# A third column group with seven products in the second eighth of an MLP, and its sums of activations in two parts

## The chip, the cores and the metric

The kernel runs on one core of one Trainium2 chip. The metric is the device time of one execution in microseconds. Before the change it is 2023.43 us, the median of three runs (2023.22 to 2023.98).

## The reference, cut to what matters

A trunk of two layers on 256 tokens of width 2048, all in float32. The change lies in the MLP that ends each layer:

```python
h2 = rms_norm(x, norm2_g[l])
x = x + jnp.square(jax.nn.relu(h2 @ w_up[l])) @ w_down[l]      # w_up 2048 x 8192, w_down 8192 x 2048
```

## The kernel before, in words

**Precision.** Every operand of a product stands as a high part (rounded to fp32r) and a low part (what is left). A product is three multiplications on TensorE: high by high, high by low, low by high. For weights, ScalarE makes the high part (`high`, L168, for a half tile L186) and VectorE the low part (`low`, L178 and L191). Weight tiles are 128 x 1024 numbers, loaded by SP into `raw` (7 buffers); `hi` and `lo` have 6 buffers each.

**The MLP in eighths.** The 8192 hidden columns are worked in eight parts of 1024. Eighth e first does w_up for its own 1024 columns: four blocks of 256 columns, each block in four steps, 16 steps in all, numbered from 0 in this text. A block's two halves add up in one PSUM bank (`acc0` or `acc1`, by turns); `after_up` then has ScalarE take it out with a Relu (L787), square it (L790) and make its high part (L646), and VectorE its low part (L649). Then come the steps of w_down for the eighth before, whose hidden columns are ready. So "the second eighth" (e = 1) multiplies w_up for its own columns and w_down for the first eighth's.

**Seven products.** An ordinary step (`transposed`, L410) is one weight tile and 24 multiplications with 256 moving columns. For 512 output columns of one eighth of w_down that makes 4 steps. A column group in `fast` (L414 to 452, multiplications at L440) does the same in two steps by seven products of half-size blocks instead of eight. Such a seven-product step takes two weight tiles, `top` and `bottom`, and makes two more from them, `upper` and `lower`: four subtractions on VectorE (L219, L220, L223, L224), and a high and a low part of each. Its 42 multiplications go through the products in this order: top; bottom twice; upper twice; lower twice. It also needs sums of activations: `sums` (L800) forms four sums and differences of the hidden blocks on VectorE (L803 to L806) and splits them into high and low parts in `shared` (L646, L649). `sums_ready` (L435) has them recorded ahead of the step.

**Where these steps stand.** The three column groups are numbered 1, 2, 3 here (g = 0, 1, 2 in the code) and cover columns 0 to 511, 512 to 1023 and 1024 to 1535. `ORDER` and `USUAL` (L63 to 66) give, for each eighth and group, the two ordinary steps ahead of which its two seven-product steps are put; such a place is called a position below. `USUAL` is ((7, 9), (2, 3), (13, 14)). The second eighth has an entry of its own with two groups. Columns outside the groups go through ordinary steps behind step 15.

**What becomes of the results.** Group 1 stays in PSUM over all eighths. Groups 2 and 3 take three banks (the one of `acc0` and `acc1` that is not in use, `acc2`, `acc3`) and half a bank for the seventh product; behind their second step ScalarE copies the three banks to `stage` (L908), later the seventh (L894), and POOL sends them to DRAM, the first time plainly and then adding (L873). Group 1 and group 3 share the half bank of the seventh product, which ScalarE empties for group 1 by L876. Ordinary columns up to 1535 are scaled and added to x by VectorE (L768, L510), those from 1536 are kept in `rest_sums` (L771 for e = 1, else L774).

**What sets the order.** The program is written out by hand. At each step the main loop first records the high parts up to five tiles past the step's first one, then what has come due (`soon`), the low parts up to four tiles past it, further due calls (`behind`), loads, and the multiplications; then `after`, and as much of the queue of `later` as a budget allows:

```python
            high_to(done + 2 + ahead)
            run_due()
            low_to(done + 1 + ahead)
            run_due(behind)
            load_more()
            mm()
```

The engines then run their own instructions in this order. So ScalarE's L787 of a block stands behind all high parts of weights that were recorded before that block's last multiplications.

Of the kernel before, what the change touches and what calls it, by code (L numbers as in the profile page):

```python
# [29 lines left out]
F32R = mybir.dt.float32r  # L30
I32 = mybir.dt.int32
AF = mybir.ActivationFunctionType
OP = mybir.AluOpType
AX = mybir.AxisListType

P = 128
# [3 lines left out]
KC = D // P  # L40
NH = 8
# [18 lines left out]

ORDER = {1: ((7, 10), (13, 14)), 6: ((12, 15), (2, 3), (7, 8)), 7: ((7, 10), (2, 3)), 8: ()}  # L63
FINAL = (7, 7, 6)
LAST = (4, 6, 8, 10, 0, 2, 12, 14)
USUAL = ((7, 9), (2, 3), (13, 14))
# [25 lines left out]
def trunk(ctx: ExitStack, tc: tile.TileContext, layout, xT, consts, gains, w, b_sp, w_sp, out):  # L92
    nc = tc.nc
# [18 lines left out]
    shared = [None]  # L112
    ar = tp.tile([P, sum(a[1] * a[2] for a in ARENA.values()) - FIRST], F32, name="ar")
    inner_flat = ar[:, 0:2048]
    inner = inner_flat.rearrange("p (k t) -> p k t", k=NH)
# [3 lines left out]
    def new_shared(dtype):  # L119

        shared[0] = tp.tile([P, FIRST], dtype, name="shared", tag="shared", bufs=1)
# [106 lines left out]
    cols = cp.tile([P, (2 * DEPTH + 1) * KC + 2 * DEPTH * NH], F32, name="cols")  # L228
# [14 lines left out]
    def later(delay, cost, fn):  # L243

        queue.append((now[0] + delay, cost, fn))
# [118 lines left out]
    summed, sum_parts = [True], [None]  # L364
# [4 lines left out]
    def collect(fn, *args, **kw):  # L369
        n = len(steps)  # L370
        fn(*args, **kw)
        part = steps[n:]
        del steps[n:]
        return part
# [100 lines left out]
    def mark(fn):  # L475

        steps.append((None, fn, None))
# [4 lines left out]
    def from_tiles(tiles, n):  # L482
        return lambda k: tiles[k // n][0][:, k % n, :, :]

    def new_half(cell):
        cell[0] = tp.tile([P, NH, 2, S], F32R, name="half", tag="half", bufs=2)
# [15 lines left out]
    def pair(ps):  # L502
        return ps.rearrange("p (a b) -> p a b", a=2)
# [14 lines left out]
    def layer(l, n1, n2, n3, last):  # L518
# [125 lines left out]
        def to_half(t, c, src, wait=False):  # L644

            act.activation(t[:, c:c + 2, 0, :], src, AF.Copy)  # L646

            def low():
                vec.tensor_tensor(t[:, c:c + 2, 1, :], src, t[:, c:c + 2, 0, :].bitcast(F32), op=OP.subtract)  # L649

            if wait:
                behind.append((now[0] + 1, low))
            else:
                low()
# [98 lines left out]
        def wide(t):  # L753
            return t[:, None, :].to_broadcast([P, 2, S])
# [8 lines left out]
        def after_down(e, c, ps):  # L763

            if e == 8:
                update(n3, c, ps, True, last)
            elif c < 12:
                vec.tensor_tensor(pair(ps), pair(ps), wide(n2.R2), op=OP.mult)  # L768
                update(n3, c, ps, False, last)
            elif e == 1:  # L770
                act.activation(rest_sums[:, c - 12:c - 10, :], pair(ps), AF.Copy)  # L771
            else:
                y = rest_sums[:, c - 12:c - 10, :]
                vec.tensor_tensor(y, y, pair(ps), op=OP.add)  # L774
# [6 lines left out]
        def after_up(e):  # L781
            def f(c, ps):
                if hid[e][0] is None:
                    new_half(hid[e])
                z = inner[:, c // P:c // P + 2, :]
                if e < 7:
                    act.activation(z, pair(ps), AF.Relu)  # L787
                else:
                    vec.scalar_tensor_tensor(z, pair(ps), 0.0, wide(n2.R), op0=OP.max, op1=OP.mult)
                act.activation(z, z, AF.Square)  # L790
                to_half(hid[e][0], c // P, z, True)
                if c == 768:
                    summed[0] = False
                    if e == 0:
                        new_shared(F32R)
                        sum_parts[0] = shared[0].rearrange("p (k h t) -> p k h t", k=NH, h=2)
                    later(1, 1.5, sums)
            return f

        def sums():  # L800

            a11, a12, a21, a22 = (inner[:, 4 * k:4 * k + 4, t * P:(t + 1) * P] for t in range(2) for k in range(2))
            vec.tensor_tensor(a22, a21, a22, op=OP.add)  # L803
            vec.tensor_tensor(a21, a11, a21, op=OP.subtract)
            vec.tensor_tensor(a11, a22, a11, op=OP.subtract)
            vec.tensor_tensor(a12, a12, a11, op=OP.subtract)  # L806

            def parts(k):
                to_half(sum_parts[0], k, inner[:, k:k + 2, :])
                summed[0] = k == 6  # L810

            for k in range(0, 8, 2):
                later(0, 0.6, lambda k=k: parts(k))

        def combine(place, c, banks, o=None):

# [46 lines left out]
        def slots_other(g, banks):  # L863
            seventh = sevenths()[g - 1]
            banks[:] = [acc_bank(1 - bank_at[0]), acc_bank(2), acc_bank(3)]
            return [h for b in banks for h in halves(b)] + [seventh]

        far = [dp.tile([P, 256 if g == 0 else 7 * 256], F32, name=f"far{l}{g}") for g in range(3)]

        def put(e, g, r):  # L870

            src = stage[:, r] if g else stage_one
            nc.gpsimd.dma_start(far[g][:, r], src, **({} if e == max(g, 1) else {"accum_op": OP.add}))  # L873

        def seventh_out(e, o):
            act.activation(stage_one, o[6], AF.Copy)  # L876
            put(e, 0, slice(0, 256))

        def first_done(e):
            def f(o):  # L880
                if e < 7:
                    soon(5, lambda: seventh_out(e, o))
                else:
                    soon(10, lambda: nc.gpsimd.dma_start(stage[:, 1536:1792], far[0]))
                    soon(15, lambda: combine(stage, 0, [aux_bank] * 2, o))
                    for i, c in enumerate((12, 14)):
                        soon(17 + 2 * i, lambda c=c: rest_in(c))
            return f

        def other_done(e, g, banks):  # L890
            here = [lambda i=i: acc_bank(i) for i in (2, 3)]

            def rest(o):
                act.activation(stage[:, 1536:1792], o[6], AF.Copy)  # L894
                for i in range(4):
                    soon(2 * i, lambda r=slice(512 * i, min(512 * (i + 1), 1792)): move(r))
                if e == FINAL[g]:
                    soon(9, lambda: combine(stage, 4 * g, here))

            def move(r):  # L900
                if e < FINAL[g]:
                    put(e, g, r)
                else:
                    nc.gpsimd.dma_start(stage[:, r], far[g][:, r], accum_op=OP.add)

            def f(o):
                for i in range(3):
                    act.activation(stage[:, 512 * i:512 * (i + 1)], banks[i], AF.Copy)  # L908
                soon(5, lambda: rest(o))
            return f  # L910

        base = len(steps)
        for e in range(9):
            up, down, quick = [], [], []
            if e == 8:
                mark(lambda: bank_at.__setitem__(0, 1))
            if e < 8:
                up = collect(transposed, "w_up", l, 0, KC, e * 1024, 1024, from_hs, after_up(e), of=2)
            if e:
                w = 512 * len(ORDER.get(e, USUAL))  # L920
                hidden = [hid[e - 1]]
                down = collect(transposed, "w_down", l, (e - 1) * 1024, 8, w, D - w, from_tiles(hidden, NH),
                               lambda c, ps, e=e, w=w: after_down(e, (c + w) // P, ps),
                               apart=last and e == 8, of=2 if e < 8 else 4,
                               cols=None if e < 8 else [c * P for c in LAST])
                for g, at in enumerate(ORDER.get(e, USUAL)):
                    banks = []
                    quick += zip(at, collect(fast, "w_down", l, (e - 1) * 1024, 512 * g, hidden,
                                             (lambda g=g, banks=banks: slots_other(g, banks)) if g else slots_first,
                                             (0, 2, 4, 6) if g or e == 1 else (6,), range(7) if g or e == 7 else (6,),  # L930
                                             other_done(e, g, banks) if g else first_done(e)))
            quick = dict(quick)
            for i, one in enumerate(up + down):
                if i in quick:
                    steps.append(quick[i])
                steps.append(one)
# [13 lines left out]
    for l in range(DEPTH):  # L950
        layer(l, norms[2 * l], norms[2 * l + 1], norms[2 * l + 2], l == DEPTH - 1)
# [80 lines left out]
    n = norms[-1]  # L1032
# [3 lines left out]
    for c, w in [(0, 1), (1, 1)] + [(c, 2) for c in range(2, KC, 2)]:  # L1036
        r = slice(c, c + w)
# [38 lines left out]
```

## Time and profile before

| | us |
|---|---|
| median of three runs | 2023.43 |
| the profiled execution | 2023.7 |
| its span, first to last instruction | 2021.9 |
| TensorE busy | 2009.5 |
| VectorE busy | 1579.8 |
| ScalarE busy | 1221.2 |

In the profile PE is TensorE (its multiplications overlap, so that one is listed longer than its distance to the next), PEld its weight loads, DVE VectorE, ACT ScalarE, POOL GpSimd. "L178" is a line of the kernel. In a row of a timeline stand the start, the length, engine, line, operation, what it writes and reads, the count, and in brackets how long the engine was idle before and what ended that.

### The profile page before, as it was taken

To read this page: it belongs to the slowest core of one execution; us is meant where nothing else is said; L and a number is where in the kernel's file an instruction comes from. 1 tells how busy PE (TensorE), PEld (TensorE's weight loads), DVE (VectorE), ACT (ScalarE), POOL (GpSimd) and SP (SyncE) were. 2 spreads that over 40 slices of the span, in tenths; PEclk is the share of its full clock that TensorE was granted. 3 is DMA by queue.
4 is the path that set the end of the run, shared out by engine and by line. 5 is a ranking of instruction groups with operands and counts; after the bars stand their busy time and mean duration, and the time that the engine had idled before them with its cause. 6 is when DMAs were issued, how large, how long until landed. Compare 5 with 4: busy or idle time off the path is not lost.

```text
span 2021.9 us, 40716 instructions
## 1 busy us (share of the span) xinstructions
PE 2009.5 (99%) x16810; PEld 1973.4 (98%) x16810; DVE 1579.8 (78%) x1954; ACT 1221.2 (60%) x1613; POOL 156.2 (8%) x200
## 2 busy tenths in 40 slices
PE   9999999999999999999999999999999999999997
PEld 8998999999999999999989989999999999999997
DVE  7566766688888898898856667667888898888985
ACT  7565455566566666665645654556666666667653
POOL 0002300000001000100000032000000000010000
PEclk9999999999999999999999999999999999999998
DMA  9555556566678776866664555565676776777662
GB/s 330 192 167 167 187 189 202 174 229 204 222 219 239 240 225 203 249 215 215 201 215 158 168 187 188 188 199 179 217 229 208 228 236 216 239 220 241 212 215 81
DMA packets 126442, 419.26 MB, mean 207 GB/s; under 512 B 14128, under 2 KB 22064, under 8 KB 126256
## 3 DMA queue, kind: packets, MB, share of 16 engines
q1 hardware_dynamic: 110800, 389.86, 57.2%
q0 software_dynamic: 14304, 23.86, 6.5%
q8 instruction: 131, 2.15, 0.4%
q10 hardware_dynamic: 1152, 2.94, 0.4%
q14 instruction: 55, 0.45, 0.1%
HBM read 394.58 MB, written 22.02 MB: 206 GB/s over the span
## 4 chain that ended last, share of the span: by engine, by line
PE 99%; DVE 0%; ACT 0%; issue 0%; DVEq 0%
PE acc L410 70%; PE acc L440 10%; PE aux L440 8%; PE acc L470 3%; PE acc L472 3%; PE acc L471 3%; PE aux L699 0%; PE aux L635 0%; PE aux L593 0%; PE aux L622 0%; PE aux L994 0%; DVE x L1038 0%; PE aux L596 0%; PE aux L637 0%; PE acc L846 0%; PE aux L539 0%
## 5 line engine op out<-in xcount | busy, mean ns | idle before, releaser
L168 ACT ACTIVATE hi<-raw 128x1024 fp32r<-128x1024 f32 (+1 forms) x817 | 836.9, 1050 | 487.5 <-DVE raw L220 216.2
L178 DVE TENSOR_TENSOR lo<-raw,hi 128x1024 fp32r<-128x1024 f32 (+1 forms) x817 | 965.3, 1214 | 143.4 <-ACT hi L168 140.4
L410 PE MATMUL acc<-hs,hi 128*128 128x256 f32 x5632 | 985.9, 277 | 0.0
L410 PEld LDWEIGHTS acc<-hs,hi 128*128 128x128 f32 x5632 | 857.9, 188 | 0.4 <-issue 0.2
L410 PE MATMUL acc<-hs,lo 128*128 128x256 f32 x2816 | 778.0, 276 | 0.0
L410 PEld LDWEIGHTS acc<-hs,lo 128*128 128x128 f32 x2816 | 528.7, 188 | 0.4 <-issue 0.2
L410 PE MATMUL acc<-half,hi 128*128 128x256 f32 x2688 | 462.2, 276 | 0.0
L410 PEld LDWEIGHTS acc<-half,hi 128*128 128x128 f32 x2688 | 406.7, 188 | 0.0
L410 PE MATMUL acc<-half,lo 128*128 128x256 f32 x1344 | 371.0, 276 | 0.0
L410 PEld LDWEIGHTS acc<-half,lo 128*128 128x128 f32 x1344 | 252.3, 188 | 0.0
L873 POOL DMA_DIRECT2D far<-ar x92 | 74.2, 816 | 1164.4 <-ACT ar L876 563.9
L440 PE MATMUL acc<-hi,shared 128*128 128x256 f32 x768 | 138.4, 276 | 0.0
L440 PEld LDWEIGHTS acc<-hi,shared 128*128 128x128 f32 x768 | 119.2, 188 | 0.0
L440 PE MATMUL aux<-hi,half 128*128 128x256 f32 x528 | 110.6, 276 | 0.0
L440 PE MATMUL acc<-lo,shared 128*128 128x256 f32 x384 | 106.0, 276 | 0.0
L649 DVE TENSOR_TENSOR half<-ar,half 128x512 fp32r<-128x512 f32 x72 | 49.8, 691 | 68.6 <-ACT half L646 68.6
L470 PE MATMUL acc<-hi,hs 128*128 128x512 f32 x256 | 101.8, 398 | 0.0
L472 PE MATMUL acc<-hi,hs 128*128 128x512 f32 x256 | 100.6, 393 | 0.0
L471 PE MATMUL acc<-lo,hs 128*128 128x512 f32 x256 | 100.3, 392 | 0.0
L440 PEld LDWEIGHTS aux<-hi,half 128*128 128x128 f32 x528 | 87.2, 188 | 0.0
L440 PE MATMUL aux<-hi,shared 128*128 128x256 f32 x448 | 80.7, 276 | 0.0
L510 DVE TENSOR_TENSOR x<-x,acc 128x512 f32<-128x512 f32 (+1 forms) x49 | 33.1, 675 | 59.1 <-PE acc L410 57.3
(150 smaller groups left out, 1955.3 us busy)
## 6 DMA issues: line engine op xcount, KB each, us to landing
raw<-in_w SPq DMA_DIRECT2D x731, 512.0 KB, 4.7
far<-ar POOLq DMA_DIRECT2D x60, 256.0 KB, 8.3
far<-ar POOLq DMA_DIRECT2D x32, 128.0 KB, 4.3
ar<-far POOLq DMA_DIRECT2D x12, 256.0 KB, 9.7
raw<-in_w SPq DMA_DIRECT2D x10, 256.0 KB, 5.1
x<-in_xT SPq DMA_DIRECT2D x7, 256.0 KB, 5.9
out<-x SPq DMA_DIRECT2D x7, 256.0 KB, 3.1
shared<-in_b_sp ACTq DMA_DIRECT2D x2, 512.0 KB, 7.7
```

The costliest lines, as they stand in the source:

```text
L168: act.activation(self.h[:, j * m:(j + 1) * m], self.raw[:, j * m:(j + 1) * m], AF.Copy)
L178: vec.tensor_tensor(lo[:, r], self.raw[:, r], self.h[:, r].bitcast(F32), op=OP.subtract)
L410: pe.matmul(o, lhsT=lhs, rhs=xs[:, rhs, :], start=(first and j == 0), stop=(last and j == 2), skip_group_check=True)
L440: calls.append(lambda k=k, j=j, lhs=lhs, rhs=rhs: pe.matmul(o[n], lhsT=lhs, rhs=rhs, start=(p == 0 and k == 0 and j == 0 and n in fresh), ...
L470: pe.matmul(ps, lhsT=xh, rhs=hi, start=(k0 + k == 0), stop=False)
L471: pe.matmul(ps, lhsT=xh, rhs=lo, start=False, stop=False)
L472: pe.matmul(ps, lhsT=xl, rhs=hi, start=False, stop=(k0 + k == KC - 1))
L510: vec.tensor_tensor(xj, xj, ps[j][:, 0:S] if alone else pair(ps)[:, j, :], op=OP.add)
L649: vec.tensor_tensor(t[:, c:c + 2, 1, :], src, t[:, c:c + 2, 0, :].bitcast(F32), op=OP.subtract)
L873: nc.gpsimd.dma_start(far[g][:, r], src, **({} if e == max(g, 1) else {"accum_op": OP.add}))
```

## The change

`ORDER` has three groups for the second eighth, at (9, 11), (5, 6) and (13, 14); before there were two, at (7, 10) and (13, 14). Its ordinary columns of w_down shrink from 1024 to 512. Group 3's first transfer to DRAM now happens in the second eighth. In the first eighth the blocks of w_up come in the order 0, 512, 256, 768; the sums of activations are formed in two parts: one behind block 512, from blocks 0 and 512, and one behind block 768, from the other two.

```diff
-ORDER = {1: ((7, 10), (13, 14)), 6: ((12, 15), (2, 3), (7, 8)), 7: ((7, 10), (2, 3)), 8: ()}
+ORDER = {1: ((9, 11), (5, 6), (13, 14)), 6: ((12, 15), (2, 3), (7, 8)), 7: ((7, 10), (2, 3)), 8: ()}
@@ after_up
                 to_half(hid[e][0], c // P, z, True)
+                if e == 0 and c == 512:
+                    new_shared(F32R)
+                    sum_parts[0] = shared[0].rearrange("p (k h t) -> p k h t", k=NH, h=2)
+                    later(1, 1.0, lambda: sums([0]))
                 if c == 768:
                     summed[0] = False
-                    if e == 0:
-                        new_shared(F32R)
-                        sum_parts[0] = shared[0].rearrange("p (k h t) -> p k h t", k=NH, h=2)
-                    later(1, 1.5, sums)
+                    later(1, 1.5, lambda: sums([0, 1] if e else [1]))
-        def sums():
-            a11, a12, a21, a22 = (inner[:, 4 * k:4 * k + 4, t * P:(t + 1) * P] for t in range(2) for k in range(2))
+        def sums(ps):
+            n, i = 2 * len(ps), 2 * ps[0]
+            a11, a12, a21, a22 = (inner[:, 4 * k + i:4 * k + i + n, t * P:(t + 1) * P] for t in range(2) for k in range(2))
@@ sums
             for k in range(0, 8, 2):
-                later(0, 0.6, lambda k=k: parts(k))
+                if k % 4 // 2 in ps:
+                    later(0, 0.6, lambda k=k: parts(k))
@@ put
-            nc.gpsimd.dma_start(far[g][:, r], src, **({} if e == max(g, 1) else {"accum_op": OP.add}))
+            nc.gpsimd.dma_start(far[g][:, r], src, **({} if e == 1 else {"accum_op": OP.add}))
@@ the loop over eighths
-                up = collect(transposed, "w_up", l, 0, KC, e * 1024, 1024, from_hs, after_up(e), of=2)
+                up = collect(transposed, "w_up", l, 0, KC, e * 1024, 1024, from_hs, after_up(e), of=2,
+                             cols=None if e else (0, 512, 256, 768))
```

VectorE at the turn from the first to the second eighth of layer 0, from the last operation of four on the sums to the last subtraction for the first seven-product step (`lo` are low parts of weights, `half` of activations, `shared` of their sums). Before:

```order
L806 TENSOR_TENSOR ar<-ar 128x4x128
L178 TENSOR_TENSOR lo<-raw,hi 128x1024
L649 TENSOR_TENSOR shared<-ar,shared 128x2x256 x2
L178 TENSOR_TENSOR lo<-raw,hi 128x1024
L649 TENSOR_TENSOR shared<-ar,shared 128x2x256 x2
L191 TENSOR_TENSOR lo<-raw,hi 128x512
L178 TENSOR_TENSOR lo<-raw,hi 128x1024
L219 TENSOR_TENSOR raw<-raw 128x2x256
```

And now, with all four operations on the second half of the sums:

```order
L805 TENSOR_TENSOR ar<-ar 128x2x128
L806 TENSOR_TENSOR ar<-ar 128x2x128
L807 TENSOR_TENSOR ar<-ar 128x2x128
L808 TENSOR_TENSOR ar<-ar 128x2x128
L191 TENSOR_TENSOR lo<-raw,hi 128x512
L649 TENSOR_TENSOR shared<-ar,shared 128x2x256 x2
L178 TENSOR_TENSOR lo<-raw,hi 128x1024
L219 TENSOR_TENSOR raw<-raw 128x2x256
```

The operations on the sums are half as wide, two of the four pairs of low parts have moved ahead, and two ordinary tiles (L178) fewer stand before the step's own.

ScalarE in the same eighth, from the `lower` tile of one seven-product step to what follows the four high parts of position 13 (the numbers tell the tiles apart; L186 is the `top` of position 13; `acc1` is the bank of columns 512 to 767 of w_up; L876, now L879, empties the seventh product of group 1). Before, behind position 10:

```order
L168 ACTIVATE hi_4565<-raw_4306 128x1024
L168 ACTIVATE hi_4597<-raw_4406 128x1024
L168 ACTIVATE hi_4627<-raw_4436 128x1024
L168 ACTIVATE hi_4673<-raw_4466 128x1024
L186 ACTIVATE hi_4675<-raw_4532 128x512
L168 ACTIVATE hi_4677<-raw_4534 128x1024
L168 ACTIVATE hi_4689<-raw_4532 128x1024
L168 ACTIVATE hi_4723<-raw_4534 128x1024
L876 ACTIVATE ar_80<-aux_4471 128x256
L787 ACTIVATE ar_80<-acc1_4572 128x512
```

And now, behind position 11:

```order
L168 ACTIVATE hi_4738<-raw_4578 128x1024
L168 ACTIVATE hi_4774<-raw_4580 128x1024
L168 ACTIVATE hi_4804<-raw_4613 128x1024
L186 ACTIVATE hi_4850<-raw_4648 128x512
L168 ACTIVATE hi_4852<-raw_4680 128x1024
L168 ACTIVATE hi_4862<-raw_4648 128x1024
L168 ACTIVATE hi_4866<-raw_4680 128x1024
L787 ACTIVATE ar_80<-acc1_4650 128x512
L790 ACTIVATE ar_80<-ar_80 128x512
L646 ACTIVATE half_4370<-ar_80 128x2x256
L168 ACTIVATE hi_4903<-raw_4744 128x1024
L879 ACTIVATE ar_80<-aux_4415 128x256
```

Two ordinary tiles instead of three now stand between the two seven-product steps, and the copy of group 1's seventh product has moved from ahead of L787 to behind it.

## The prediction

> **What bounds the kernel now.** I read the page first, then TensorE's waits, then the busy time stage by stage, then the engines' timelines around the second eighth of the MLP. The page has the span, the engines and the chain that ended last.
>
> ```profile
> span 2021.9 us, 40716 instructions
> PE 2009.5 (99%) x16810; PEld 1973.4 (98%) x16810; DVE 1579.8 (78%) x1954; ACT 1221.2 (60%) x1613; POOL 156.2 (8%) x200
> PE 99%; DVE 0%; ACT 0%; issue 0%; DVEq 0%
> ```
>
> TensorE is the chain. The view of waits, for TensorE alone, has two rows, both outside the MLP's eighths:
>
> ```profile
> PE aux L328 <- DVE nr L354: 1.2, 1, 1.2
> PE aux L994 <- DVE warm L990: 1.1, 1, 1.1
> ```
>
> So the kernel's time is the number of multiplications times their pace, and an edit can gain only by removing multiplications, and lose only by making TensorE wait. Busy time by stage (columns: stretch, length, PE, PEld, DVE, ACT, POOL, granted clock, DMA share, GB/s), for the first eighth, the second, and the third of layer 0:
>
> ```profile
> 333.20:376.80 43.60, 43.60 (x386) 43.60 (x385) 26.14 (x36) 23.62 (x31) 0.00 (x0) 1.00 0.60 193
> 376.80:461.10 84.30, 84.30 (x745) 84.30 (x744) 71.98 (x84) 54.50 (x69) 2.96 (x5) 1.00 0.59 201
> 461.10:544.20 83.10, 83.10 (x735) 83.10 (x734) 69.48 (x78) 54.41 (x69) 6.60 (x9) 1.00 0.72 227
> ```
>
> The second eighth, which has seven products in two column groups, lasts 84.3 us; the third, which has them in all three, 83.1. TensorE is busy throughout all three at full clock. VectorE has slack in the first eighth (26 of 43.6 us) and little later (72 of 84).
>
> **What is removed.** Group 3 costs 4 ordinary steps of 24 multiplications, 96, before; now 2 seven-product steps of 42, 84. That is 12 fewer in each layer, 24 in all. Their pace, from the first seven-product multiplication of the third eighth and of the fourth, in TensorE's timeline:
>
> ```profile
> 466.44 0.28 PE L440 MATMUL acc<-hi,half 128*128 128x256 f32 x1
> 549.52 0.28 PE L440 MATMUL acc<-hi,half 128*128 128x256 f32 x1
> ```
>
> One eighth with three groups is (16 + 4) x 24 + 6 x 42 = 732 multiplications, and 83.08 / 732 = 0.1135 us each. So 24 x 0.1135 = 2.72 us go, 1.36 in each layer. An ordinary step takes 2.72 us, a seven-product step 4.77.
>
> The Trainium skill (TensorE: Matmul & The Clock Gate, "Wait — 56ns, not 53.3ns?") puts the distance of warm multiplications at N / 2.4 GHz plus about 2.5 ns. By that, an estimate from that page, 256 columns take 109.2 ns and the change removes 2.62 us; the trace has 113.5 ns, so the measurement decides.
>
> **What is added beside TensorE, and where it lies.** Each seven-product step needs, from VectorE, low parts of four weight tiles and four subtractions, and from ScalarE four high parts. Group 3's two steps cost VectorE more than its four ordinary tiles did, so VectorE's work per stretch is the matter. In the third eighth (the nearest row of an eighth with three groups) its work for one such step and what follows reads:
>
> ```profile
> 490.90 1.23 DVE L178 TENSOR_TENSOR lo<-raw,hi 128x1024 fp32r<-128x1024 f32 x1 [0.20 <-ACT hi L168]
> 492.04 0.68 DVE L191 TENSOR_TENSOR lo<-raw,hi 128x512 fp32r<-128x512 f32 x1
> 492.94 1.23 DVE L178 TENSOR_TENSOR lo<-raw,hi 128x1024 fp32r<-128x1024 f32 x1 [0.21 <-ACT hi L168]
> 494.08 0.68 DVE L219 TENSOR_TENSOR raw<-raw 128x512 f32<-128x512 f32 x1
> 494.80 0.69 DVE L220 TENSOR_TENSOR raw<-raw 128x512 f32<-128x512 f32 x1
> 495.52 0.69 DVE L223 TENSOR_TENSOR raw<-raw 128x512 f32<-128x512 f32 x1
> 496.25 0.69 DVE L224 TENSOR_TENSOR raw<-raw 128x512 f32<-128x512 f32 x1
> 496.86 2.52 DVE L178 TENSOR_TENSOR lo<-raw,hi 128x1024 fp32r<-128x1024 f32 x2
> 499.97 0.69 DVE L649 TENSOR_TENSOR half<-ar,half 128x512 fp32r<-128x512 f32 x1 [0.59 <-ACT half L646]
> 500.92 4.63 DVE L178 TENSOR_TENSOR lo<-raw,hi 128x1024 fp32r<-128x1024 f32 x4 [0.26 <-ACT hi L168]
> ...
> 517.01 0.69 DVE L191 TENSOR_TENSOR lo<-raw,hi 128x512 fp32r<-128x512 f32 x1
> ...
> 521.53 4.77 DVE L178 TENSOR_TENSOR lo<-raw,hi 128x1024 fp32r<-128x1024 f32 x4
> ```
>
> From the top's low part (492.04) to the end of lower's (499.38) are 7.34 us, 0.29 of it a wait; without it 7.05, which I take (top 0.61, bottom 1.14, subtractions 2.78, upper and lower 2.52). The step at 517.01 took 6.9. An ordinary tile takes 1.14. So from position 9 to 15, with four seven-product and seven ordinary steps, VectorE has 4 x 7.05 + 7 x 1.14 + 2 x 0.69 = 37.6 us of work, and TensorE 4 x 4.77 + 7 x 2.72 = 38.1. There is next to no room for waits there; before, only three seven-product steps (10, 13, 14) lay in that stretch.
>
> **First place: the sums, position 5.** TensorE starts the second eighth at 376.8 and now reaches its first seven-product step at 376.8 + 5 x 2.72 = 390.4, where before it was position 7. ScalarE, then VectorE, at that place before, and a 256-wide VectorE operation:
>
> ```profile
> 376.80 0.60 ACT L787 ACTIVATE ar<-acc 128x512 f32<-128x512 f32 x1 [1.66 <-PE acc L410]
> 378.63 2.00 ACT L168 ACTIVATE hi<-raw 128x1024 fp32r<-128x1024 f32 x2
> 387.68 0.60 ACT L787 ACTIVATE ar<-acc 128x512 f32<-128x512 f32 x1 [1.66 <-PE acc L410]
> ...
> 378.76 0.69 DVE L649 TENSOR_TENSOR half<-ar,half 128x512 fp32r<-128x512 f32 x1 [2.36 <-ACT half L646]
> 392.08 3.49 DVE L178 TENSOR_TENSOR lo<-raw,hi 128x1024 fp32r<-128x1024 f32 x3
> ...
> L826 DVE TENSOR_TENSOR ar<-ar 128x256 f32<-128x256 f32 x6 | 2.5, 417 | 0.0
> ```
>
> Half of the sums is now done in the first eighth, in VectorE's slack, at no cost. The rest, from 379.45: four 256-wide operations (0.45 each with the gap) to 381.3, the top's low part 381.9, two low parts of sums 383.2, bottom 384.3, subtractions 387.1, upper 388.3, lower 389.6. TensorE reads upper after 18 multiplications (392.4) and lower after 30 (393.8): 4 us in hand, so no wait. Before, upper and lower came out of the row at 392.08, for a step at 395.8: as much in hand. The bank that the step takes is free when ScalarE's L787 is through, about 388.9: 1.5 us in hand.
>
> **Second place: ScalarE between positions 6 and 13.** Behind group 2, ScalarE copies three banks and cannot get on with weights until TensorE is through. That is shown in the third eighth behind position 3, which ended at 478.7:
>
> ```profile
> 478.22 0.60 ACT L908 ACTIVATE ar<-acc 128x512 f32<-128x512 f32 x1 [0.76 <-PE acc L440]
> 478.72 2.00 ACT L168 ACTIVATE hi<-raw 128x1024 fp32r<-128x1024 f32 x2
> 480.62 0.62 ACT L186 ACTIVATE hi<-raw 128x512 fp32r<-128x512 f32 x1
> 486.24 0.37 ACT L894 ACTIVATE ar<-aux 128x256 f32<-128x256 f32 x1
> ...
> 497.06 1.06 ACT L168 ACTIVATE hi<-raw 128x1024 fp32r<-128x1024 f32 x1 [0.39 <-DVE raw L224]
> 498.02 0.58 ACT L787 ACTIVATE ar<-acc 128x512 f32<-128x512 f32 x1
> 498.63 0.64 ACT L790 ACTIVATE ar<-ar 128x512 f32<-128x512 f32 x1
> 499.30 0.63 ACT L646 ACTIVATE half<-ar 128x512 fp32r<-128x512 f32 x1
> 499.84 3.89 ACT L168 ACTIVATE hi<-raw 128x1024 fp32r<-128x1024 f32 x4
> 512.96 0.60 ACT L787 ACTIVATE ar<-acc 128x512 f32<-128x512 f32 x1 [1.61 <-PE acc L410]
> ...
> 479.81 2.36 DVE L178 TENSOR_TENSOR lo<-raw,hi 128x1024 fp32r<-128x1024 f32 x2 [2.62 <-ACT hi L168]
> ```
>
> VectorE stood for 2.62 us and started again 1.1 us behind the step's end. Call that end R. There, four ordinary steps lie between this and the next seven-product step; now it is three (6, 7, 8), then 9, 11, 13 and 14. TensorE gets to position 9 at R + 8.2, to 11 at 18.4, to 13 at 28.6, to 14 at 36.1. VectorE's side:
>
> Step 8's tile ends at 2.25, position 9's four at 9.3; lower is read at 11.6: 2.3 in hand. ScalarE's lower (7.0) is followed by a copy (0.3), L787, L790, L646 (497.06 to 499.84 is 2.78 for a weight tile and these three), so step 9's weights start there at 10.1, and VectorE (1.08 later, as from 499.84 to 500.92) ends at 12.3; read at 12.9: 0.6 in hand. Step 10 ends at 13.45, position 11's upper at 19.15 (read at 20.4), lower at 20.5. Steps 11 and 12 end at 22.75, position 13's subtractions at 27.3. Now ScalarE's lower high part runs from 27.4 to 28.35, and only then L787 of columns 512 to 767, which empties the bank that group 3's first product takes: to 28.95. TensorE is there at 28.6. It waits 0.35, with the handover 0.4. In the third eighth L787 itself waited for TensorE (512.96), so nothing waited for it. Behind it step 13's tile ends at 32.45 (read at 33.8), position 14's upper at 38.2 (read at 38.5): 0.3 in hand. Then the order is that of later eighths.
>
> So each layer gains 1.36 and loses 0.4. The wait's bounds: with 6.9 us for each of the three seven-product steps ahead, VectorE is 0.45 earlier and the wait is gone; with 7.34 it is 0.87 later and the wait 1.3. I take 0.4, by the 7.05 of rows without waits.
>
> **At nothing.** Four more bank copies per layer on ScalarE are in the walk above. Four more transfers per layer are issued on POOL, busy 3 of 84 us there. SP's loads keep number and order; a weight buffer is loaded again seven loads later, over 10 us, and no TensorE wait for weights is in the rows above. The vector updates of columns 1024 to 1535 (four operations per layer) go, behind position 15, where nothing waits for them. Turning the first eighth's blocks moves the same 384 multiplications. If VectorE's slack there were gone, the half sums would cost up to their 4 x 0.45 us, but 17 us are idle.
>
> **Sum.** The profiled execution took 2023.7 (span 2021.9 and 1.8 around it), 0.3 over the median, 2023.43. 2 x (1.36 - 0.4) = 1.9: 2021.8 for such an execution, 2021.5 against the median. About 0.2% (4.0 us) is what a measurement of this kernel can tell from no change; all of the removed work is less than that.
>
> **Rivals.**
> No wait (0.25): VectorE is half a microsecond earlier, L787 is through in time, the whole 2.72 shows: 2020.7. For it: TensorE waits nowhere in any eighth now. Against it: no eighth has this spacing.
> VectorE falls behind (0.20), the one that ends slower: at positions 9, 11 and 13 it waits for ScalarE as at 499.97 and 500.92 (0.59 + 0.26 us), 2.5 us in all; all of it adds to the lateness at position 13, 0.4 + 2.5 = 2.9 us in each layer: 2023.43 - 2.72 + 5.8 = 2026.5. It decides from 1.36 us per layer (slower than before), and from 3.4 it passes 0.2%. For it: 37.6 us of work in 38.1. Against it: some of these waits are in the walk already.
> The Trainium skill (same page, "Part 1: The HAM clock gate") states that TensorE falls to half clock after an idle window of about 3.4 us. The granted clock was 1.00 in each stage above; by an estimate from that page a wait beyond that would cost another 1.7 us, which no run here shows yet.
> It does not do what it says (0.05): another wait eats just what is gained, 2023.4.
>
> **Numbers.** The forecast (a wait of 0.1 to 1.3 per layer, 2021.0 to 2023.3) has 0.50. The range runs from 2020.4 (no wait, less the runs' spread of 0.2 to 0.3) to 2024.2, into the first third of VectorE's case; it leaves out some 0.15. Faster by over 0.2% needs more than all removed work: 0.01. Slower by over 0.2%: the far quarter of VectorE's case, 0.05. Within: 0.94.
>
> **What would show it.** Right: 24 fewer multiplications; the second eighth at about 83.3 us; TensorE's waits have a row at L440 or L410 behind ScalarE's L787 near position 13, 0.4 us in each layer; none at position 5. Wrong: a wait at position 5 on the sums; waits on L178 at 9, 11 or 14 of more than 1.3 us; a third eighth longer than 83.1.

## The result, and the profile after

The changed kernel takes 2054.98 us (median of 5 runs, 2053.74 to 2055.56); the kernel before took 2023.6 beside it (2023.22 to 2023.98). The ratio is 1.0155, with an interval of 1.0141 to 1.0168: 31.4 us slower, where the prediction had 2 us faster. The profiled execution took 2054.98, its span 2053.2.

The page and TensorE's waits look like those of before. The page's span, engines and granted clock, then the one row that is new in the view of waits (PEld are weight loads; the columns are us in total, times, longest; the view of before has no row at L440, and the view of the multiplications alone, PE, has the same two rows as before, since the wait stands at a weight load):

```profile
span 2053.2 us, 40733 instructions
PE 2040.8 (99%) x16786; PEld 2004.3 (98%) x16786; DVE 1595.6 (78%) x1978; ACT 1233.7 (60%) x1629; POOL 162.8 (8%) x208
PEclk9999999999999999999999999999999999999999
```

```profile
PEld acc L440 <- ACT ar L787: 0.6, 2, 0.3
```

There are 24 multiplications fewer (16786 for 16810), one new wait of 0.3 us in each layer, at a seven-product step behind ScalarE's L787, and a granted clock at 0.9 or more throughout. Yet TensorE is busy for 31.3 us longer. Nothing in these views says where. The busy time by stage does, in the same columns as before (first eighth and third):

```profile
333.40:377.00 43.60, 43.60 (x386) 43.60 (x385) 28.89 (x42) 24.71 (x33) 0.00 (x0) 1.00 0.62 195
...
460.80:547.10 86.30, 86.30 (x735) 86.30 (x734) 72.33 (x82) 55.66 (x70) 7.82 (x9) 1.00 0.73 218
```

The first eighth takes the same 43.60 us for the same 386 multiplications. The third takes 86.30 for 735, where before it took 83.10 for 735. The clock is 1.00 in both. So each multiplication takes longer, with nothing to wait for. Grouped by operation over one stretch of 10 us (500 to 510), before and after, with the mean length in ns last ahead of the idle time:

```profile
L410 PE MATMUL acc<-hs,hi 128*128 128x256 f32 x32 | 5.7, 276 | 0.0
```

```profile
L410 PE MATMUL acc<-hs,hi 128*128 128x256 f32 x30 | 5.6, 281 | 0.0
```

The chain in order of time (start, length, what) shows from where to where. A stretch of ordinary multiplications divided by its count gives the pace. Before, in the third eighth:

```profile
478.99 10.78 PE acc L410 x95
```

After, from the start of layer 0's MLP to its end (rows are left out in between; L849, before L846, are the transposes that `turn_back` makes in the eighth eighth; "turned blocks" below):

```profile
341.61 48.98 PE acc L410 x432
480.05 11.20 PE acc L410 x95
566.34 11.20 PE acc L410 x95
849.28 11.20 PE acc L410 x95
884.53 0.44 PE acc L849 x4
890.87 8.18 PE acc L410 x72
```

48.98 / 432 is 113.4 ns. Then 11.20 / 95 is 117.9, the same from the third eighth to the eighth, and behind the turned blocks (four transposes at 884.53, four more at 890.43) it is 8.18 / 72 = 113.6 again. TensorE's timeline at position 13 of the second eighth has the place where it begins (rows that hold two multiplications are left out), and ScalarE's timeline what it waited for:

```profile
430.74 0.28 PE L410 MATMUL acc<-hs,lo 128*128 128x256 f32 x1
431.08 0.28 PE L410 MATMUL acc<-hs,lo 128*128 128x256 f32 x1
431.19 0.28 PE L410 MATMUL acc<-hs,hi 128*128 128x256 f32 x1
431.59 0.39 PE L440 MATMUL acc<-hi,half 128*128 128x256 f32 x1
431.81 0.28 PE L440 MATMUL acc<-lo,half 128*128 128x256 f32 x1
432.17 0.28 PE L440 MATMUL acc<-lo,half 128*128 128x256 f32 x1
432.52 0.28 PE L440 MATMUL acc<-lo,half 128*128 128x256 f32 x1
```

```profile
429.99 1.06 ACT L168 ACTIVATE hi<-raw 128x1024 fp32r<-128x1024 f32 x1 [0.39 <-DVE raw L224]
430.96 0.58 ACT L787 ACTIVATE ar<-acc 128x512 f32<-128x512 f32 x1
```

Every third multiplication, the one with a low part of the weights, has a row of its own here. Up to 431.08 these stand 0.34 us apart, from 431.81 on 0.35 to 0.36. Between lies the predicted wait: 431.19 + 0.11 would be 431.30, and TensorE starts at 431.59, when L787 (done at 431.54) has freed the bank.

So the 31 us are a slower pace from that wait to the turned blocks, in each layer: one eighth is 566.34 - 480.05 = 86.29 us, 3.21 over the 83.08 of before. From position 13 of the second eighth to the first turned blocks are about 3,843 multiplications, 5.25 eighths of 732, so 16.9 us in each layer and 33.7 in both. Less the 2.7 removed and with 0.6 of wait, that makes 31.6; the medians differ by 31.4.

### The profile page after: what moved, and what is told of

It reads as the page before. It is cut to its first block, busy times and chain, and to the rows that moved or that the text cites. A ratio compares the mean times of both kernels' runs of the same rounds, so it can differ in the third digit from the quotient of the medians.

```text
span 2053.2 us, 40733 instructions
## 1 busy us (share of the span) xinstructions
PE 2040.8 (99%) x16786; PEld 2004.3 (98%) x16786; DVE 1595.6 (78%) x1978; ACT 1233.7 (60%) x1629; POOL 162.8 (8%) x208
## 4 chain that ended last, share of the span: by engine, by line
PE 96%; DVE 2%; ACT 1%; issue 1%; DVEq 0%; ACTq 0%
PE acc L410 67%; PE acc L440 11%; PE aux L440 7%; PE acc L470 3%; PE acc L472 3%; PE acc L471 3%; ACT hi L168 1%; DVE lo L178 0%; PE aux L699 0%; PE aux L635 0%; PE aux L593 0%; PE aux L622 0%; PE aux L998 0%; DVE x L1042 0%; DVE raw L224 0%
## 5 line engine op out<-in xcount | busy, mean ns | idle before, releaser
L178 DVE TENSOR_TENSOR lo<-raw,hi 128x1024 fp32r<-128x1024 f32 (+1 forms) x821 | 970.3, 1214 | 153.2 <-ACT hi L168 149.7
L410 PE MATMUL acc<-hs,hi 128*128 128x256 f32 x5632 | 1003.8, 279 | 0.0
L410 PE MATMUL acc<-half,hi 128*128 128x256 f32 x2560 | 444.9, 278 | 0.0
L410 PEld LDWEIGHTS acc<-half,hi 128*128 128x128 f32 x2560 | 388.6, 188 | 0.0
L410 PE MATMUL acc<-half,lo 128*128 128x256 f32 x1280 | 355.0, 277 | 0.0
L410 PEld LDWEIGHTS acc<-half,lo 128*128 128x128 f32 x1280 | 241.7, 189 | 0.0
L876 POOL DMA_DIRECT2D far<-ar x100 | 80.7, 810 | 1187.4 <-ACT ar L911 772.1
L440 PE MATMUL acc<-hi,shared 128*128 128x256 f32 x832 | 154.5, 279 | 0.0
L440 PEld LDWEIGHTS acc<-hi,shared 128*128 128x128 f32 x832 | 130.4, 188 | 0.0
L440 PE MATMUL aux<-hi,half 128*128 128x256 f32 x544 | 116.5, 279 | 0.0
L440 PE MATMUL acc<-lo,shared 128*128 128x256 f32 x416 | 115.9, 279 | 0.0
L440 PEld LDWEIGHTS aux<-hi,half 128*128 128x128 f32 x544 | 90.4, 188 | 0.0
L440 PE MATMUL aux<-hi,shared 128*128 128x256 f32 x448 | 82.8, 278 | 0.0
L440 PE MATMUL acc<-hi,half 128*128 128x256 f32 x416 | 81.8, 280 | 0.2
```

Source lines behind the costliest of these rows:

```text
L178: vec.tensor_tensor(lo[:, r], self.raw[:, r], self.h[:, r].bitcast(F32), op=OP.subtract)
L410: pe.matmul(o, lhsT=lhs, rhs=xs[:, rhs, :], start=(first and j == 0), stop=(last and j == 2), skip_group_check=True)
L440: calls.append(lambda k=k, j=j, lhs=lhs, rhs=rhs: pe.matmul(o[n], lhsT=lhs, rhs=rhs, start=(p == 0 and k == 0 and j == 0 and n in fresh), ...
L876: nc.gpsimd.dma_start(far[g][:, r], src, **({} if e == 1 else {"accum_op": OP.add}))
```

## The experiments

The theory (the first in the expectations): TensorE runs these multiplications at either of two paces. A standstill sets the slower one, and it stays until multiplications of another kind come, as the transposes of the turned blocks are. The rival: it is the added work (a third seven-product group in the second eighth, the sums in two parts, what VectorE, ScalarE and the transfers do beside TensorE) that slows each multiplication. The expectations are quoted as they stood before each run.

**The third group later, no wait.**

```diff
-ORDER = {1: ((9, 11), (5, 6), (13, 14)), 6: ((12, 15), (2, 3), (7, 8)), 7: ((7, 10), (2, 3)), 8: ()}
+ORDER = {1: ((9, 11), (5, 6), (14, 15)), 6: ((12, 15), (2, 3), (7, 8)), 7: ((7, 10), (2, 3)), 8: ()}
```

> The changed kernel with group 3 at positions 14 and 15 of the second eighth in place of 13 and 14, nothing else. ScalarE's L787 is then through 2.3 us before TensorE wants the bank. Theory 1 (a standstill of TensorE leaves it at a slower pace, 117.8 ns for a multiplication of 256 columns in place of 113.3, until multiplications of another kind come): no wait, no slower pace, 2023.6 less 2.7: 2020.9 us. Theory 2 (the third group's work for VectorE, ScalarE and POOL in the second eighth, or the order of the groups and the sums in two parts, slow the multiplications): that work is all still there, so 2050 to 2055 us with multiplications at 117.8 ns.

Measured: 2020.48 us (2019.83 to 2021.17), ratio to before 0.9986 (0.9977 to 0.9995); span 2018.6. The weight loads' waits have no row at L440, and the chain of this run has the step itself and the third eighth at the faster pace:

```profile
434.13 4.08 PE acc L440 x36
477.83 10.78 PE acc L410 x95
```

All the added work is still there, one step later, and the time is 34.5 us shorter. The rival falls. The difference to before, 3.0 us, is the 2.72 of the removed multiplications within the runs' spread. This kernel beats both.

**The kernel before with a wait.** Five copies of a constant onto itself on ScalarE, ahead of L787 of columns 512 to 767 in the second eighth; nothing of the change.

```diff
+                if e == 1 and c == 512:
+                    for _ in range(5):
+                        act.activation(con[:, 0:512], con[:, 0:512], AF.Copy)
```

> The kernel before, with five more copies of 512 columns on ScalarE (a constant onto itself) ahead of L787 of columns 512 to 767 in the second eighth of each layer, so that TensorE has to wait some 0.4 us for the bank at position 13. TensorE's program is that of before. Theory 1: 117.8 ns from position 13 on to the first turned blocks in the eighth eighth, some 3850 multiplications a layer, 2 x 17 us: 2055 to 2059 us. Theory 2: 2024 to 2026 us, the waits alone.

Measured: 2060.03 us (2059.8 to 2060.4), ratio 1.0181 (1.0167 to 1.0195). The wait (L790 in this run is the L787 of before) and the chain:

```profile
PEld acc L440 <- ACT ar L790: 1.9, 2, 1.0
```

```profile
482.19 11.20 PE acc L410 x95
913.57 10.78 PE acc L410 x95
```

A wait of 0.9 to 1.0 us in each layer costs 36.6 us in all. Twice the wait is 1.9; the rest, 34.7, is 17.3 in each layer. From position 13 to the turned blocks this kernel has 96 multiplications more than the changed one (512 more ordinary columns, four steps of 24), and 3,939 x 4.4 ns is 17.3. The change isn't needed for it.

**Transposes behind the wait.** The changed kernel, with four transposes into the awaited bank ahead of group 3's first product (how `e` gets there is left out).

```diff
+            if e == 1 and g == 2:
+                for j in range(4):
+                    pe.transpose(banks[0][:, j * P:(j + 1) * P], con[:, j * P:(j + 1) * P], ident)
```

> The changed kernel with four transposes of 128 columns put between the wait at position 13 of the second eighth and group 3's first product, into the bank that this product then overwrites. The wait stays, and four transposes (0.45 us) are added in each layer. Theory 1: the pace behind the transposes is 113.3 ns, as it is behind the turned blocks of the eighth eighth: 2023.6 - 2.7 + 0.6 + 0.9 = 2022.4 us. Theory 2: 2055 to 2056 us.

Measured: 2055.48 us (2054.85 to 2056.08), ratio 1.0159 (1.0143 to 1.0176). A miss: the transposes took over the wait (row at L871 of 0.3 us in each layer), and behind them the pace was the slower one. The timeline and the chain:

```profile
431.53 0.66 PE L871 MATMUL acc<-con 128*128 128x128 f32 x4
432.15 0.28 PE L440 MATMUL acc<-lo,half 128*128 128x256 f32 x1
432.50 0.28 PE L440 MATMUL acc<-lo,half 128*128 128x256 f32 x1
```

```profile
480.37 11.19 PE acc L410 x95
```

So transposes as such don't bring the faster pace back. Either they can't do so right behind a wait, or it matters into what TensorE goes from them: here a seven-product step, at the turned blocks an ordinary one.

**The sums alone.** The kernel before with the sums in two parts and the turned order of blocks, and the two groups of before.

```diff
-                    later(1, 1.5, sums)
+                    later(1, 1.5, lambda: sums([0, 1] if e else [1]))
...
+                             cols=None if e else (0, 512, 256, 768))
```

> The kernel before with the sums in two parts and the first eighth's blocks in turned order alone; two groups in the second eighth, at the old positions. Both theories, if the change of the sums has no price of its own: 2023.6 us. If the sums or the turned order are the cause of the slower pace: 2050 us and more.

Measured: 2023.6 us (2023.0 to 2024.34), ratio 1.0001 (0.999 to 1.0011). This part of the change costs nothing by itself.

**A wait later in the layer.** The kernel before with seven copies in the sixth eighth, so that less of the layer is left.

```diff
+                if e == 5 and c == 512:
+                    for _ in range(7):
+                        act.activation(con[:, 0:512], con[:, 0:512], AF.Copy)
```

> The kernel before, with seven copies of 512 columns on ScalarE ahead of L787 of columns 512 to 767, this time in the sixth eighth, so that TensorE waits 0.3 to 1 us at position 13 there. From that point to the first turned blocks some 920 multiplications are left in each layer, against 3850 from the second eighth. Theory 1 (a wait at the entry of a seven-product step leaves the slower pace until the turned blocks): 2 x 920 x 4.45 ns = 8.2 us and the waits of 0.6 to 2: 2032 to 2034 us. A price that goes with each wait or with the load alone: 2024 to 2026; one that hangs on the whole MLP: 2055 and more.

Measured: 2033.57 us (2033.1 to 2033.58), ratio 1.0049 (1.0033 to 1.0065). The chain holds the whole story in a few rows:

```profile
728.64 10.78 PE acc L410 x95
...
765.50 0.49 ACT ar L790
...
814.48 11.19 PE acc L410 x95
...
873.72 0.44 PE acc L849 x4
...
888.23 4.08 PE acc L440 x36
```

The faster pace, the awaited L790 behind the copies, the slower pace, the turned blocks, the faster pace. 914 multiplications of each layer run at the slower one: 2 x (914 x 4.4 ns + 0.9) = 9.8 us, measured 9.9. The loss is the length of what is left up to the turned blocks, not the length of the wait.

**A wait at an ordinary step, first try.** The kernel before with 16 copies ahead of the first L787 of the first eighth, where the next multiplications are ordinary.

```diff
+                if e == 0 and c == 0:
+                    for _ in range(16):
+                        act.activation(con[:, 0:512], con[:, 0:512], AF.Copy)
```

> The kernel before, with sixteen copies of 512 columns on ScalarE behind the first block of the first eighth, so that weights come late by 0.5 to 3 us for an ordinary step there, where no seven-product step is near. Theory 1 in its wide form (any standstill): 117.8 ns from there to the turned blocks, some 4500 multiplications a layer: 2064 to 2070 us. In its narrow form (only a standstill ahead of a seven-product step, whose stationary operand is the activations): the waits alone, 2025 to 2030 us, at 113.3 ns.

Measured: 2023.87 us (2023.63 to 2024.33), ratio 1.0002 (0.9992 to 1.0012). Inconclusive: the copies came to an end just in time, TensorE was held up by some 0.2 us, and the views of waits have no row for it. The pace stayed at 113.4.

**Transposes without a wait.** The kernel before with the four transposes ahead of the first product at position 13 of the second eighth, where the bank had long been free (how `e` gets there is left out).

```diff
+            if e == 1 and g == 1:
+                for j in range(4):
+                    pe.transpose(banks[0][:, j * P:(j + 1) * P], con[:, j * P:(j + 1) * P], ident)
```

> The kernel before, with four transposes of 128 columns ahead of the first product at position 13 of the second eighth, into the bank that it then overwrites; ScalarE is through with that bank 2 us ahead, so there is no wait. In the changed kernel such transposes behind the wait did not bring the faster pace. If the standstill sets the pace: 113.3 ns, 2023.6 + 0.9 = 2024.5 us. If going over to a seven-product step from anything but running 256-column multiplications sets it: 117.8 ns from there on, 2055 to 2058 us.

Measured: 2058.29 us (2057.8 to 2058.78), ratio 1.0172 (1.0151 to 1.0192). TensorE's timeline, ScalarE's L787 and the chain:

```profile
421.78 0.28 PE L410 MATMUL acc<-hs,hi 128*128 128x256 f32 x1
421.90 0.60 PE L868 MATMUL acc<-con 128*128 128x128 f32 x4
```

```profile
419.38 0.60 ACT L787 ACTIVATE ar<-acc 128x512 f32<-128x512 f32 x1 [0.27 <-PE acc L410]
```

```profile
422.50 4.24 PE acc L440 x36
481.98 11.19 PE acc L410 x95
```

L787 was done at 419.98 and the transposes began at 421.90, 0.12 behind the multiplication ahead of them: no wait. The step's 36 multiplications take 4.24 us all the same, where the kernel with the third group one step later took 4.08 for 36, and the pace stays. So the theory falls in part: no standstill is needed. At this place, to come into a seven-product step from four transposes is enough.

**Transposes ahead of an ordinary step.** The changed kernel, wait and all, with four transposes ahead of ordinary step 1 of the third eighth, into a bank that the step doesn't use (`four_turns` has the four transposes of the experiments above).

```diff
+                if e == 2 and i == 1:
+                    mark(lambda: four_turns(acc_bank(2)))
```

> The changed kernel, with four transposes of 128 columns ahead of ordinary step 1 of the third eighth in each layer, into a free bank. The wait at position 13 of the second eighth stays. If transposes ahead of an ordinary step bring back 113.3 ns, as they seem to in the eighth eighth: the slow stretch is 290 multiplications a layer: 2023.6 - 2.7 + 0.6 + 0.9 + 2.6 = 2025.0 us. If the slower pace has a cause that stays (the load of the third group, the order of groups): 2055 to 2057 us.

Measured: 2028.47 us (2027.85 to 2029.01), ratio 1.0024 (1.0014 to 1.0034). The chain of layer 0:

```profile
441.47 4.24 PE acc L440 x36
...
466.22 0.44 PE acc L917 x4
...
469.39 4.08 PE acc L440 x36
```

4.24 us for 36 multiplications ahead of the transposes, 4.08 behind them. Four transposes, 0.44 us, bring the faster pace back for 3,566 multiplications, and 26.5 of the 31.4 us. The time is 3.5 us above the expected 2025.0. The rest lies elsewhere in this kernel: its blocks of w_in ahead of the attention run at the slower pace,

```profile
81.97 11.31 PE acc L410 x96
93.94 11.31 PE acc L410 x96
```

though their instructions on TensorE are those of before. Before, only the first of them did (its rows are shown further down). Four such blocks at 0.41 us and half a one at 0.20 make 1.8 us in each layer, 3.7 in both: all of the rest. Why they changed is not settled.

**A wait at an ordinary step, longer.** As above, with 20 copies.

```diff
-                    for _ in range(16):
+                    for _ in range(20):
```

> As the run with sixteen copies, whose wait ahead of an ordinary step of the first eighth came out at 0.2 us only; now with twenty copies, so that it is 2 to 3 us in each layer. If any standstill leaves the slower pace: 2064 us and more. If only the entry of a seven-product step does: the waits alone, 2 x 2.5 on top of 2023.6, 2028 to 2030 us, at 113.3 ns.

Measured: two executions, 2049.91 and 2070.75 us; ratio 1.0182 (1.0135 to 1.0229). The profiled one is that of 2049.91. The row of its waits behind the copies, and its timeline in layer 1:

```profile
PEld acc L410 <- ACT ar L790: 4.2, 2, 2.1
```

```profile
1360.90 0.38 PE L410 MATMUL acc<-hs,hi 128*128 128x256 f32 x1 [1.89 <-ACT ar L790]
...
1364.44 0.39 PE L410 MATMUL acc<-hs,lo 128*128 128x256 f32 x1 [0.42 <-DVE lo L178]
```

And the third eighth of both layers in its chain:

```profile
482.52 10.78 PE acc L410 x95
1490.57 11.20 PE acc L410 x95
```

Layer 0, with one wait of 2.1 us, went on at the faster pace (its clock was halved for some 3.4 us first; see the last section). Layer 1 went on at the faster pace behind the same wait, and at the slower one behind a second, short one, 3.5 us later, inside a step. So behind a wait among ordinary multiplications either can follow. The other execution is 20.8 us longer, about what a whole layer at the slower pace costs (some 4,500 multiplications x 4.4 ns = 20); that it was layer 0's is argued, not traced.

**The groups without the two-part sums.** The kernel before with three groups in the second eighth, each later than in the change (group 2 by two steps, the others by one), and the sums in one piece.

```diff
-ORDER = {1: ((7, 10), (13, 14)), 6: ((12, 15), (2, 3), (7, 8)), 7: ((7, 10), (2, 3)), 8: ()}
+ORDER = {1: ((10, 12), (7, 8), (14, 15)), 6: ((12, 15), (2, 3), (7, 8)), 7: ((7, 10), (2, 3)), 8: ()}
...
-            nc.gpsimd.dma_start(far[g][:, r], src, **({} if e == max(g, 1) else {"accum_op": OP.add}))
+            nc.gpsimd.dma_start(far[g][:, r], src, **({} if e == 1 else {"accum_op": OP.add}))
```

> One part of the change alone: three groups in the second eighth, with the sums in one piece and the first eighth's blocks in the old order; positions (10, 12), (7, 8) and (14, 15), where by the walk along ScalarE and VectorE no wait comes up (0.6 us in hand at the closest place, position 10). Theory 1: 2023.6 less 2.7: 2020.9 us at 113.3 ns; with a wait at position 10 after all, 2054 us. If the sums in two parts bring part of the gain: over 2022 us.

Measured: 2020.63 us (2019.97 to 2021.04), ratio 0.9985 (0.9976 to 0.9994), the same as with the two-part sums.

The whole gain comes from the third group; the new handling of the sums isn't needed for it at these positions. Whether position 5 could do without it was not run.

**Taken together.** Ahead of a seven-product step, all eight waits traced (0.3 to 1.0 us) and all four entries from transposes were followed by the slower pace. Ahead of an ordinary step of the MLP, turned blocks and added transposes were followed by the faster one, and waits by either. The transposes differ in more than the step that follows: ahead of the seven-product step they wrote into the bank that its first product takes, ahead of the ordinary step into another. No run separates the two. And blocks of w_in, entered from other multiplications, had either pace, as shown further down.

## Why the prediction was wrong, by its steps

**What is removed: right.** 24 multiplications went, and where nothing else changes (the two kernels with the later third group) the time falls by 3.0 us, against 2.72 worked out.

**The sums, position 5: right.** No wait came there. The new handling is free, as said; at the old positions it is also without effect.

**ScalarE ahead of position 13: right, in place and size.** L787 behind the four high parts, 0.4 us in each layer predicted, 0.3 measured. Positions 9, 11 and 14 got no wait, so the rival that VectorE falls behind is out: no row with L178 at these steps appeared.

**What bounds the kernel: wrong, and this is the step that failed.** "So the kernel's time is the number of multiplications times their pace, and an edit can gain only by removing multiplications, and lose only by making TensorE wait." The pace was taken for a constant, "0.1135 us each". It has two values, 113.4 and 117.8 ns, and the wait that I priced at its own length picked the slower one for all that followed: 16.9 us in each layer behind 0.3 us. The cost that I gave to a wait was right only for the time in which TensorE stands.

The profile of before held the second value. Its chain in order of time, for the first and the third block of w_in in layer 0, each with what runs ahead of it:

```profile
81.44 0.44 PE aux L596 x4
81.88 11.31 PE acc L410 x96
...
106.91 0.44 PE aux L596 x4
107.36 10.90 PE acc L410 x96
```

The same line with the same count takes 11.31 us and then 10.90, 117.8 and 113.5 ns, and both blocks come behind the same four multiplications of L596. So what runs directly ahead doesn't settle the pace by itself. I read the pace from one eighth and didn't ask whether the other stretches had it. With both values seen, a rival could have been put up, though nothing in that profile shows that a wait picks the slower one: a wait at position 13 and the slower pace up to the turned blocks, 2023.43 - 2.72 + 33.7 + 0.6 = 2055.0.

**What was to show it.** The listed sign of an error, "a third eighth longer than 83.1", did appear (86.30), but for a cause that no rival had. The second eighth took 84.4 us (377.0 to 461.4 in TensorE's timeline), not 83.3: the 252 multiplications from position 13 to its end, at 4.4 ns more each, are 1.1 of it.

**The clock gate.** It isn't that: the granted clock is 1.00 in the slow stretches. The Trainium skill (TensorE: Matmul & The Clock Gate, "Part 1: The HAM clock gate") has a full and a half rate, and a limit of 13/16 that it ties to three busy cores of a die; a step of 4% in the pace is none of them. By its N / 2.4 GHz plus 2.5 ns (same page of the Trainium skill, "Wait — 56ns, not 53.3ns?") an estimate for 256 columns is 109.2 ns, below both paces measured.

**Open.** What in TensorE makes the two paces and what selects one on entry stays open. The views show only that the distance of starts, and the length of a multiplication in the records (276 and 281 ns), change together. Why w_in's blocks changed theirs in one experiment is open, too.

## What to carry to other kernels

Where one engine is the chain, work out its pace (length over count) for several equal stretches, before and after; where the same work shows two values, a change may move stretches from one to the other, and here neither waits nor busy shares nor the granted clock told. A wait can then cost more than its length: here its price was what ran behind it, up to the next thing that reset the pace. Here the remedy was to put the step one position later, where its bank is free in time.

## What the runs showed of the hardware that was not expected

Back-to-back fp32r multiplications of 256 columns, each with its own weights, ran at 113.4 or at 117.8 ns at a granted clock of 1.00, and kept a pace over thousands: 3,843 in each layer of the changed kernel.

The half clock appeared, too. In the run with 20 copies, busy time by stage around the wait of layer 0 and behind that of layer 1 (the clock is the third figure from the end):

```profile
357.40:359.80 2.40, 2.40 (x13) 2.40 (x13) 1.60 (x2) 2.40 (x4) 0.00 (x0) 0.50 0.00 0
361.00:363.00 2.00, 2.00 (x20) 2.00 (x19) 2.00 (x3) 1.94 (x4) 0.00 (x0) 1.00 0.83 268
1361.00:1364.00 3.00, 3.00 (x25) 2.83 (x25) 1.53 (x2) 2.95 (x4) 0.00 (x0) 1.00 0.00 0
```

Behind a wait of 2.1 us the clock was 0.50 for about 3.4 us in layer 0, from some 0.7 us after TensorE had started again (in its timeline three multiplications take 0.64 us there and 0.34 right after), and 1.00 in layer 1 behind a wait just as long. The prediction's sentence from the Trainium skill put an idle window of about 3.4 us before this; here a wait of 2.1 was followed by it, once of two times.
